# The first half's mix of two softmax maps: one DVE instruction, or a multiplication on ACT and an addition on POOL

## The chip, the cores and the metric

The kernel runs on one core of a Trainium2 chip. The core has five engines with queues of their own: PE (matrix products), DVE (vector), ACT (activations), POOL (general) and SP (here for DMA issues). An engine runs its instructions in the order in which they were issued to it, and waits on semaphores for what other engines produce. The metric is the device time of one execution in microseconds, as the median of several runs.

## The reference, cut to what matters

The block has two layers. Each projects 2048 latent and 256 context tokens, runs four mixers side by side (differential attention, HGRN2, windowed attention, mLSTM) and projects back. The change lies in the differential attention: 4 heads, and for each of them two softmax maps over all 2304 keys, which are subtracted before they meet the values:

```python
def attend(qs, ks, vs):
    s = jnp.einsum('mbhqd,mbhkd->mbhqk', qs, ks).astype(F32) * scale
    p = jax.nn.softmax(s, axis=-1)
    w = (p[0] - lam * p[1]).astype(vs.dtype)
    return jnp.einsum('bhqk,bhkv->bhqv', w, vs)

nb = n_tok // ATTN_QBLOCK
qb = jnp.moveaxis(q.reshape(2, b, DA_HEADS, nb, ATTN_QBLOCK, DA_QK), 3, 0)
o = lax.map(lambda qq: attend(qq, keys, vals), qb)
```

## The kernel before

A **unit** is 128 query rows of one head. There are 64 latent units in each layer, and in layer 0 also 8 context units over 256 keys. The 2304 keys of a latent unit are two halves: j = 0 with 1024 and j = 1 with 1280 columns (`HALF`). For each map m, first 1 and then 0:

- `diff_scores` has PE write the scores of a half into PSUM (`scr`), and DVE reduce it to its minimum (L1048). From the two minima DVE makes the bias of the map, called the **bound** here: for m = 1 a TENSOR_TENSOR of two columns of `sm` (in the trace under the helper's line, L108, as `sm<-sm 128x1`), for m = 0 a TENSOR_SCALAR (L1056).
- `diff_exp` has ACT take the exponential of both halves out of PSUM into `p`, with the row sums as accumulator (L105).
- `diff_mix`, for the unit before (`u1`), puts the maps together: j = 0 behind the bound of m = 1, j = 1 behind the bound of m = 0 (`tc.issue_after`). The factor `sm[:, 14:15]` comes out of three small DVE operations (L1073 to L1075). The mix itself was one DVE SCALAR_TENSOR_TENSOR, p1 * factor + p0 (L111). ACT casts the result to f16 (L1084), POOL subtracts that from the f32 value, which gives the low part (L108), and SP transposes both by DMA into `wt` (L1087).
- `diff_out` and `diff_norm` multiply `wt` with the values on PE, one and two units later, and normalise.

There is one score tile for each half (`sc0`, `sc1`, one buffer each), so PE can write the scores of the next map's half only when ACT has read the exponential of this half. Between them `pump` lets the projections of the other mixers run as filler on PE: `FSTEP` ns of it between the two halves' scores, `FGAP` behind the second. PE's order is written out by hand (`manual_schedule`); on DVE, ACT and POOL a scheduler sets the order of mix, exponentials, reductions and the filler's evictions.

A unit has two **rounds**: A from the bound of m = 1 to the bound of m = 0, B from there to the next unit's bound of m = 1.

Of the kernel before, what the change touches and what calls it, by code (L numbers as in the profile page):

```python
# [14 lines left out]
AF = mybir.ActivationFunctionType  # L15
ALU = mybir.AluOpType
# [57 lines left out]
def kernel(  # L74
# [8 lines left out]
    V, A, G, PE, SP = nc.vector, nc.scalar, nc.gpsimd, nc.tensor, nc.sync  # L83
# [20 lines left out]
    def act(o, i, f, **kw):  # L104
        A.activation(out=o, in_=i, func=f, **kw)  # L105

    def tt(e, o, a, b, op):
        return e.tensor_tensor(out=o, in0=a, in1=b, op=op)  # L108

    def stt(o, a, s, b, op0, op1):  # L110
        V.scalar_tensor_tensor(out=o, in0=a, scalar=s, in1=b, op0=op0, op1=op1)  # L111
# [146 lines left out]
    for l in range(n_layers):  # L258
# [83 lines left out]
        with tc.tile_pool(name=f"pa{l}", bufs=2, reuse_waits="tile", side="right" if l else "left") as pa, tc.tile_pool(name=f"pap{l}", bufs=4, space=PSUM, reuse_waits="tile") as pap:  # L342
# [53 lines left out]
            for gi, g in enumerate(gorder):  # L396
                g0, gn_ = GROUPS[g]
                n = gn_ // P
# [629 lines left out]
        with ExitStack() as st2:  # L1028
# [4 lines left out]
            def halves_of(u):  # L1033
                return [(2048, 256)] if u["ctx"] else HALF
# [33 lines left out]
            def diff_mix(u, j):  # L1068

                sm = u["sm"]  # L1070
                if j == 0:
                    zs = sm[:, 6:10].rearrange("p (m j) -> p m j", j=2)[:, :, :len(halves_of(u))]
                    V.tensor_reduce(sm[:, 10:12], zs, AX.X, ALU.add)  # L1073
                    V.reciprocal(sm[:, 12:14], sm[:, 10:12])
                    V.tensor_scalar(sm[:, 14:15], sm[:, 10:11], sm[:, 13:14], nlam, ALU.mult, ALU.mult)  # L1075
                    u["w"] = []
                hs = halves_of(u)
                if j >= len(hs):
                    return
                k0, n = hs[j]  # L1080
                p = u[1][j]
                stt(p[:, :n], p[:, :n], sm[:, 14:15], u[0][j][:, :n], ALU.mult, ALU.add)
                wl = u[0][j].bitcast(F16)
                A.copy(wl[:, :n], p[:, :n])  # L1084
                tt(G, wl[:, n:2 * n], p[:, :n], wl[:, :n], ALU.subtract)
                wt = da.tile([P, 20, P], F16, tag="wt", name="wt")
                SP.dma_start_transpose(wt[:, :2 * (n // P)], wl[:, :2 * n])  # L1087
                u["w"].append(wt)
# [80 lines left out]
            with tc.manual_schedule(engines=MANUAL):  # L1169
                while True:  # L1170
                    u = next(it, None)
                    if u is None and u1 is None and u2 is None and u3 is None:
                        break
                    if u:
                        diff_scores(u, 1)
                    if u3:
                        diff_out(u3, 1)
                    pump(FGAP * (u["work"] if u else 1.0))
                    if u1:
                        with tc.issue_after(u["nm"].ins) if u else ExitStack():  # L1180
                            diff_mix(u1, 0)
                    if u:
                        diff_exp(u, 1)
                    if u3:
                        diff_norm(u3, 0)
                    if u:
                        diff_scores(u, 0)
                    if u3:
                        diff_norm(u3, 1)
                    if u2:  # L1190
                        diff_out(u2, 0)
                    pump(FGAP * (u["work"] if u else 1.0))
                    if u1:
                        with tc.issue_after(u["nm"].ins) if u else ExitStack():
                            diff_mix(u1, 1)
                    if u:
                        diff_exp(u, 0)
                    u1, u2, u3 = u, u1, u2
# [528 lines left out]
```

## Time and profile before

| | |
|---|---|
| median of 3 runs | 4203.35 us (4197.22 to 4208.07) |
| the profiled execution's own time | 4220.02 us |
| its span in the profile | 4218.2 us |
| DVE / ACT / POOL busy | 2873.5 / 2332.9 / 2358.5 us |
| PE busy | 3570.4 us |
| instructions | 78854 |

The span runs from the first to the last instruction of the profiled execution; its own time has some 2 us around that. Busy times are sums over instructions, those that wait for a shared resource while they run included. The first scores of the attention stage start at 237.7 us and the last at 3295.9 us, with the other mixers of layer 0 and the first blocks of layer 1 between the two layers' stages.

### The profile page before, as it was taken

The numbers are of one execution on the slowest core, as the hardware profiler recorded it, in microseconds if no ns is written. First come the engines' busy times: TensorE is split into PE (matmuls) and PEld (weight loads), VectorE is DVE, ScalarE is ACT, GpSimd is POOL, SyncE is SP. The second block draws the span as 40 slices with busy tenths as digits, with TensorE's granted clock in tenths as the row PEclk, the third lists the DMA queues.
The fourth block names the chain that finished last, engine by engine and source line by source line (L and its number), as shares of the span: only waits on it lengthen the run. The fifth ranks groups of instructions, "written<-read, shape, count | busy, mean of one in ns | idle before, by whom it ended". The sixth has DMA issues, their size and how long they took to land.

```text
span 4218.2 us, 78854 instructions
## 1 busy us (share of the span) xinstructions
PE 3570.4 (85%) x30342; PEld 2395.7 (57%) x30342; DVE 2873.5 (68%) x4550; ACT 2332.9 (55%) x4679; POOL 2358.5 (56%) x1727
## 2 busy tenths in 40 slices
PE   6988878888769987989998888788876798789998
PEld 3656655444547675556656476544444575556665
DVE  5168888888885546556643499888899766556664
ACT  5245656666655545555653366666666664555663
POOL 4443555443445458778857545645344554677883
PEclk7999989999989986888999999999998999778998
DMA  5356866667666547467754467566776662646662
GB/s 205 100 138 151 189 131 165 135 150 157 127 142 165 134 133 174 143 167 170 184 152 142 121 133 158 126 147 150 151 161 132 155 163 84 166 124 161 169 169 76
DMA packets 1256960, 622.19 MB, mean 148 GB/s; under 512 B 913476, under 2 KB 1203848, under 8 KB 1256584
## 3 DMA queue, kind: packets, MB, share of 16 engines
q1 hardware_dynamic: 1154216, 490.64, 51.2%
q10 hardware_dynamic: 102368, 126.52, 8.9%
q8 instruction: 239, 3.92, 0.4%
q14 instruction: 137, 1.12, 0.1%
HBM read 291.76 MB, written 131.23 MB: 100 GB/s over the span
## 4 chain that ended last, share of the span: by engine, by line
PE 31%; DVE 18%; POOL 8%; issue 7%; DMA 7%; ACT 5%; SPq 1%; ACTq 0%; POOLq 0%; DVEq 0%
PE fx L94 7%; PE ptm L94 5%; PE pfm L94 5%; DVE sm L1048 4%; PE go L94 4%; PE mnum L94 3%; PE scr L94 2%; ACT p L105 2%; DVE p L111 2%; POOL E L108 2%; DMA swt<-ph 1%; POOL yt L108 1%; PE gA L94 1%; PE ss L94 1%; DVE sm L108 1%
## 5 line engine op out<-in xcount | busy, mean ns | idle before, releaser
L108 POOL TENSOR_TENSOR p<-p,p 128x1024 f16<-128x1024 f32 (+2 forms) x264 | 623.4, 2362 | 793.7 <-ACT p L1084 704.4
L94 PE MATMUL ptm<-wb,hh 128*128 128x256 f16 (+2 forms) x5024 | 834.6, 273 | 30.3 <-DVE tm L111 7.4
L105 ACT ACTIVATE p<-scr,sm 128x1024 f32<-128x1024 f32 (+2 forms) x528 | 628.2, 1194 | 416.4 <-DVE sm L1073 143.3
L1048 DVE TENSOR_REDUCE sm<-scr 128x1 f32<-128x1024 f32 (+2 forms) x528 | 698.9, 1326 | 218.0 <-PE scr L94 214.2
L94 PE MATMUL pfm<-hh,wb 128*128 128x512 f16 (+1 forms) x2592 | 809.0, 376 | 26.5 <-DVE gz L111 10.4
L94 PE MATMUL ptm<-wb,hl 128*128 128x256 f16 (+2 forms) x2512 | 671.9, 273 | 1.8 <-POOL hl L108 1.8
L94 PEld LDWEIGHTS <-wb 128*128 128x128 f16 x3888 | 378.8, 101 | 410.8 <-issue 81.1
L94 PE MATMUL scr<-Ks,Qs 128*128 128x512 f16 (+1 forms) x1296 | 364.5, 380 | 289.2 <-ACT p L105 284.1
L94 PEld LDWEIGHTS <-hh 128*128 128x128 f16 x5024 | 479.0, 100 | 131.3 <-issue 37.7
L94 PE MATMUL pfm<-hl,wb 128*128 128x512 f16 (+1 forms) x1296 | 488.1, 377 | 0.0
L111 DVE SCALAR_TENSOR_TENSOR p<-p,sm,p 128x1024 f32<-128x1024 f32 (+2 forms) x264 | 414.6, 1571 | 8.2
L94 PE MATMUL fx<-wo,mh 128*128 128x512 f16 x1088 | 371.8, 426 | 6.2 <-DVE xt L111 2.7
L94 PEld LDWEIGHTS <-Qs 128*128 128x128 f16 x1296 | 130.4, 102 | 429.9 <-issue 359.5
L1084 ACT CAST p<-p 128x1024 f16<-128x1024 f32 (+2 forms) x264 | 297.4, 1126 | 40.0 <-DVE p L111 35.3
L94 PEld LDWEIGHTS <-wt 128*128 128x128 f16 x4640 | 245.1, 103 | 71.7 <-DMA wt<-p 23.6
L94 PE MATMUL pv<-Vs,wt 128*128 128x128 f16 (+1 forms) x4640 | 259.6, 214 | 22.1 <-DMA wt<-p 14.6
L94 PEld LDWEIGHTS <-hl 128*128 128x128 f16 x2512 | 250.6, 100 | 36.1 <-POOL hl L108 3.3
L94 PE MATMUL fx<-wo,mlo 128*128 128x512 f16 x544 | 230.0, 423 | 6.1 <-DVE mlo L108 5.9
L108 POOL TENSOR_TENSOR E<-lk,cm 128x512 f32<-128x512 f32 (+1 forms) x136 | 205.3, 1510 | 41.2 <-DMA cm<-dhc 19.7
L108 POOL TENSOR_TENSOR ph<-swp,ph 128x640 f16<-128x640 f32 (+2 forms) x136 | 190.7, 1402 | 59.5 <-ACT ph L1326 45.1
L108 DVE TENSOR_TENSOR QQ<-hq,E 128x512 f32<-128x512 f32 x119 | 148.1, 1253 | 73.6 <-ACT E L105 35.9
L105 ACT ACTIVATE E<-E 128x1024 f32<-128x1024 f32 x136 | 143.0, 1052 | 99.5 <-POOL E L108 93.1
(298 smaller groups left out, 6853.7 us busy)
## 6 DMA issues: line engine op xcount, KB each, us to landing
wraw<-in_w_in_dram SPq DMA_DIRECT2D x60, 512.0 KB
dgt<-ga ACTq DMA_DIRECT2D x68, 256.0 KB
r1b<-dr SPq DMA_DIRECT2D x68, 256.0 KB
gtt<-dgt SPq DMA_DIRECT2D x34, 512.0 KB
mraw<-in_w_mod_dram SPq DMA_DIRECT2D x64, 256.0 KB
vi<-dhi SPq DMA_DIRECT2D x49, 256.0 KB
KSb<-dsk SPq DMA_DIRECT2D x56, 192.0 KB
Ks<-dka SPq DMA_DIRECT2D x64, 144.0 KB
```

The lines of the kernel that those rows point to most:

```text
L94: PE.matmul(o, lhsT=lhsT, rhs=rhs, start=start, stop=stop)
L105: A.activation(out=o, in_=i, func=f, **kw)
L108: return e.tensor_tensor(out=o, in0=a, in1=b, op=op)
L111: V.scalar_tensor_tensor(out=o, in0=a, scalar=s, in1=b, op0=op0, op1=op1)
L1048: V.tensor_reduce(sm[:, m * 2 + j:m * 2 + j + 1], ps[:, :n], AX.X, ALU.min)
L1084: A.copy(wl[:, :n], p[:, :n])
```

## The change

For the first half (j = 0) of a latent unit the DVE instruction is replaced by two: ACT multiplies p1 in place by the factor (`AF.Copy` with a scale of one value per partition), and POOL adds p0 to it. Both work on 128x1024 f32 in SBUF. The second half and the context units keep the DVE instruction. It happens 128 times.

```diff
--- before.py
+++ after.py
@@ -1079,7 +1079,11 @@
                     return
                 k0, n = hs[j]
                 p = u[1][j]
-                stt(p[:, :n], p[:, :n], sm[:, 14:15], u[0][j][:, :n], ALU.mult, ALU.add)
+                if j or u["ctx"]:
+                    stt(p[:, :n], p[:, :n], sm[:, 14:15], u[0][j][:, :n], ALU.mult, ALU.add)
+                else:
+                    act(p[:, :n], p[:, :n], AF.Copy, scale=sm[:, 14:15])
+                    tt(G, p[:, :n], p[:, :n], u[0][j][:, :n], ALU.add)
                 wl = u[0][j].bitcast(F16)
                 A.copy(wl[:, :n], p[:, :n])
                 tt(G, wl[:, n:2 * n], p[:, :n], wl[:, :n], ALU.subtract)
```

In the built programs DVE loses 128 instructions, ACT and POOL gain 128 each; on PE the order is the same through both attention stages. In the stages behind them (windowed attention, mLSTM and HGRN2), where the scheduler also orders PE, pieces of the two programs' order have changed places: nothing there was edited. Names such as `p_2591` are buffers of one unit's exponentials; the numbers differ between the two programs.

ACT in layer 0, from the exponential of a unit's map 1, half 0, to the cast of the unit before, half 1. Before:

```order
L105 ACTIVATE p_2745,sm<-scr,sm 128x1024
L105 ACTIVATE p_2747,sm<-scr,sm 128x1280
L1084 CAST p_2661<-p_2588 128x1024
L638 DMA dmv_100<-tm 128x256
L105 ACTIVATE p_2830,sm<-scr,sm 128x1024
L105 ACTIVATE p_2832,sm<-scr,sm 128x1280
L1084 CAST p_2663<-p_2590 128x1280
```

The two exponentials of a map follow each other, and the cast of the unit before comes behind them. The same place in the changed kernel:

```order
L105 ACTIVATE p_2749,sm<-scr,sm 128x1024
L105 ACTIVATE p_2591<-p_2591,sm 128x1024
L105 ACTIVATE p_2751,sm<-scr,sm 128x1280
L638 DMA dmv_100<-tm 128x256
L1088 CAST p_2664<-p_2591 128x1024
L105 ACTIVATE p_2834,sm<-scr,sm 128x1024
L105 ACTIVATE p_2836,sm<-scr,sm 128x1280
L1088 CAST p_2666<-p_2593 128x1280
```

The multiplication (`p_2591<-p_2591,sm`) stands between the two exponentials of map 1, and the cast of its result comes behind the second of them. So it stands in 78 of the 128 units.

A place of the other kind, also on ACT in layer 0, in the changed kernel:

```order
L105 ACTIVATE p_7010,sm<-scr,sm 128x1024
L162 COPY mrow<-modps 128x256
L105 ACTIVATE p_7012,sm<-scr,sm 128x1280
L105 ACTIVATE p_6876<-p_6876,sm 128x1024
L105 ACTIVATE ot<-pv,sm 128x64
L105 ACTIVATE p_7061,sm<-scr,sm 128x1024
L105 ACTIVATE p_7063,sm<-scr,sm 128x1280
L162 COPY mrow<-modps 128x256
L1088 CAST p_6950<-p_6876 128x1024
L1088 CAST p_6952<-p_6878 128x1280
```

Here the multiplication (`p_6876<-p_6876,sm`) stands behind both exponentials of map 1, and the cast of its result behind the exponentials of map 0, next to the cast of the second half. So it is in 43 units; in the last 7 the cast follows the multiplication with no exponential of map 0 between them.

POOL in layer 0, the low parts of three units. Before:

```order
L108 TENSOR_TENSOR p_2361<-p_2297,p_2361 128x1024
L108 TENSOR_TENSOR p_2363<-p_2299,p_2363 128x1280
L108 TENSOR_TENSOR p_2498<-p_2418,p_2498 128x1024
L108 TENSOR_TENSOR p_2500<-p_2420,p_2500 128x1280
L108 TENSOR_TENSOR p_2661<-p_2588,p_2661 128x1024
L108 TENSOR_TENSOR p_2663<-p_2590,p_2663 128x1280
```

One subtraction of 1024 columns and one of 1280 alternate. And in the changed kernel:

```order
L108 TENSOR_TENSOR p_2420<-p_2420,p_2500 128x1024
L108 TENSOR_TENSOR p_2500<-p_2420,p_2500 128x1024
L108 TENSOR_TENSOR p_2502<-p_2422,p_2502 128x1280
L108 TENSOR_TENSOR p_2591<-p_2591,p_2664 128x1024
L108 TENSOR_TENSOR p_2664<-p_2591,p_2664 128x1024
L108 TENSOR_TENSOR p_2666<-p_2593,p_2666 128x1280
```

Each addition (`p_2591<-p_2591,p_2664`) stands ahead of the subtraction of the same half on POOL's queue.

## Rows read from the trace of the kernel before

**Rows 1.** Page, part 1: busy us of each engine, share of span, instructions.

```profile
PE 3570.4 (85%) x30342; PEld 2395.7 (57%) x30342; DVE 2873.5 (68%) x4550; ACT 2332.9 (55%) x4679; POOL 2358.5 (56%) x1727
```

**Rows 2.** Windows in the attention stage: length, busy us (instructions) by engine, clock, DMA.

```profile
800.00:1200.00 400.00, 316.22 (x2607) 195.13 (x2606) 343.52 (x545) 242.10 (x394) 169.12 (x96) 0.93 0.64 142
...
2800.00:3200.00 400.00, 321.57 (x2651) 187.74 (x2651) 351.15 (x502) 259.82 (x401) 177.99 (x93) 0.96 0.71 153
```

**Rows 3.** Waits, whole span: waiting line, releaser: us in total, times, longest.

```profile
POOL p L108 <- ACT p L1084: 704.4, 194, 12.7
...
PE scr L94 <- ACT p L105: 284.1, 190, 6.9
DVE sm L1048 <- PE scr L94: 214.2, 261, 4.7
...
ACT p L105 <- DVE sm L1056: 141.7, 68, 7.5
```

**Rows 4.** Timeline of DVE, one unit: start, duration us, line, operation, [idle before].

```profile
3022.74 0.15 DVE L108 TENSOR_TENSOR sm<-sm 128x1 f32<-128x1 f32 x1
...
3023.57 1.28 DVE L111 SCALAR_TENSOR_TENSOR p<-p,sm,p 128x1024 f32<-128x1024 f32 x1
3024.87 1.23 DVE L1048 TENSOR_REDUCE sm<-scr 128x1 f32<-128x1024 f32 x1
3026.71 1.49 DVE L1048 TENSOR_REDUCE sm<-scr 128x1 f32<-128x1280 f32 x1 [0.61 <-PE scr L94]
3028.23 0.27 DVE L1056 TENSOR_SCALAR sm<-sm,shf 128x1 f32<-128x1 f32 x1
3028.42 1.57 DVE L111 SCALAR_TENSOR_TENSOR p<-p,sm,p 128x1280 f32<-128x1280 f32 x1
...
3032.26 1.49 DVE L1048 TENSOR_REDUCE sm<-scr 128x1 f32<-128x1280 f32 x1 [0.61 <-PE scr L94]
...
3033.86 1.04 DVE L108 TENSOR_TENSOR sm<-sm 128x1 f32<-128x1 f32 x1
```

**Rows 5.** Timeline of ACT, the same unit.

```profile
3022.99 1.11 ACT L105 ACTIVATE p<-scr,sm 128x1024 f32<-128x1024 f32 x1 [0.68 <-DVE sm L1073]
...
3024.09 1.32 ACT L105 ACTIVATE p<-scr,sm 128x1280 f32<-128x1280 f32 x1
...
3025.39 1.04 ACT L1084 CAST p<-p 128x1024 f16<-128x1024 f32 x1
3026.33 0.69 ACT L105 ACTIVATE fm<-pfm,bcol 128x512 f32<-128x512 f32 x1
...
3028.54 1.12 ACT L105 ACTIVATE p<-scr,sm 128x1024 f32<-128x1024 f32 x1 [1.52 <-DVE sm L1056]
...
3029.65 1.32 ACT L105 ACTIVATE p<-scr,sm 128x1280 f32<-128x1280 f32 x1
...
3030.95 1.25 ACT L1084 CAST p<-p 128x1280 f16<-128x1280 f32 x1
```

**Rows 6.** Timeline of PE, the same unit, scores alone.

```profile
3024.24 0.59 PE L94 MATMUL scr<-Ks,Qs 128*128 128x512 f16 x2 [0.34 <-ACT p L105]
...
3025.97 0.70 PE L94 MATMUL scr<-Ks,Qs 128*128 128x512 f16 x3
```

**Rows 7.** Timeline of POOL, the same unit.

```profile
3026.51 2.13 POOL L108 TENSOR_TENSOR p<-p,p 128x1024 f16<-128x1024 f32 x1 [4.52 <-ACT p L1084]
3032.28 2.61 POOL L108 TENSOR_TENSOR p<-p,p 128x1280 f16<-128x1280 f32 x1 [3.64 <-ACT p L1084]
```

**Rows 8.** Groups by form: count, busy us, mean ns, idle us before, releasers.

```profile
L111 DVE SCALAR_TENSOR_TENSOR p<-p,sm,p 128x1024 f32<-128x1024 f32 x128 | 174.0, 1359 | 7.6
...
L1084 ACT CAST p<-p 128x1024 f16<-128x1024 f32 x128 | 133.5, 1043 | 28.0 <-DVE p L111 23.3 <-DVE gates L637 1.8 <-issue 1.4
...
L108 POOL TENSOR_TENSOR qe<-qe,hq 128x1024 f32<-128x1024 f32 x17 | 40.4, 2378 | 51.7 <-ACT qe L105 51.7
```

**Rows 9.** Tile sm: count, duration ns min/median/max, first and last start.

```profile
L108 DVE TENSOR_TENSOR sm<-sm x136: 127/773/2320, 248.7 to 3290.6; 128x1 f32<-128x1 f32 x136
```

## The prediction

> **What bounds the kernel now.** The page's first part comes first: PE is busy for 85% of the span, DVE for 68% [rows 1]. That is an average over stages, so the next view is the windows in the attention stage, where the change lies: there DVE is busy for 344 and 351 of 400 us, PE for 316 and 322, ACT for 242 and 260, POOL for 169 and 178 [rows 2]. DVE at 86 to 88% looks like the bound, and POOL looks empty. The waits say something else: DVE's reductions of the scores waited 261 times for PE, out of 528 (136 units, two maps, two halves, fewer halves for context units), and PE's scores waited 190 times, 284 us in all, for ACT's exponentials [rows 3]. So the three engines chase each other in a ring, and none is the bound alone.
>
> The ring is best seen in one unit with little filler on DVE [rows 4 to 7]. I count from the end of the bound of map 1, 3022.89. ACT starts the first exponential at 3022.99 and the second at 3024.09, which ends at 3025.41. PE's scores for the second half start at 3025.97. DVE's reduction of them starts at 3026.71, after 0.61 us of waiting for exactly these scores, and the bound of map 0 ends at 3028.50. Round A took 5.61 us, and DVE's mix (3023.57, 1.28 us) was no part of its chain: DVE was idle behind it. In round B the chain is another: ACT's exponentials end at 3030.97, the cast of the second half runs from 3030.95, POOL's subtraction from 3032.28 to 3034.89, and the bound of the next unit, a DVE operation on two SBUF columns, takes 1.04 us instead of the 0.15 us that it took one unit earlier: it ends at 3034.90, when POOL's instruction ends. Round B took 6.40 us. So POOL's subtraction holds this bound up. That is common: over the span the median of this operation is 773 ns against a minimum of 127 [rows 9].
>
> **The change, part by part.** *DVE loses* 128 mixes of 1359 ns mean [rows 8], 174 us. In the unit above that gives nothing, since the wait for scores only grows from 0.61 us. It gives something where the reduction found its scores ready, about half the time (267 of 528, by the count above), so in some 64 rounds A. There the gain lies between 0 and 1.36 us; half or more of these rounds belong to units where ACT's delay below brings the scores later anyway, so I take 0.3 us each, near the lower end: **-20 us** (bounds 0 and -87).
>
> *ACT gains* 128 multiplications of 128x1024 f32. The trace has none with a scale from a tile; the nearest row is the cast of the same tile, 1043 ns [rows 8], and back to back with the next instruction it took 0.94 us (3025.39 to 3026.33); the exponential out of PSUM took 1.11 [rows 5]. I take 1.0 us of delay (bounds 0.94 and 1.11). In 78 units the built order puts it between the two exponentials of map 1. Then the second ends at 3026.41 instead of 3025.41. PE's filler had kept the scores waiting until 3025.97 anyway; they can now start about 0.14 us behind the exponential (as the scores of 3024.24 did, whose exponential ended at 3024.10), at 3026.55. So 0.58 us of the 1.0 reaches the reduction, which already waited, and round A grows by that: 78 x 0.58 = **+45 us** (bounds: 0 if PE's filler is long enough everywhere, 78 x 1.11 = 87).
>
> The Trainium skill has a price for such an instruction (page "ScalarE: Activation LUTs", section "What ACT_TABLE_LOAD costs"): about 280 ns and 0.833 ns per column with an operand per partition, an estimate of 1133 ns for 1024 columns. No row here shows a multiplication of this kind; the exponential, with a bias per partition, agrees with 1.11 us [rows 5]. By the page the delay would be 0.09 us more than the cast's 1.04, this term 52 and the sum below 70 in place of 63.
>
> *POOL gains* 128 additions. The nearest row is an f32 product of the same shape, 2378 ns [rows 8], the subtraction with an f16 side took 2.13 [rows 7]; I take 2.38. In the 78 units: the multiplication ends at 3025.13, the addition runs from 3025.21 (0.08 us behind, as the subtraction of 3026.51 was behind its cast) to 3027.59. ACT's cast, behind the second exponential, must now wait for it and runs from 3027.65 to 3028.69, and the subtraction from 3028.77 to 3030.90. Queued behind that waiting cast on ACT are evictions of filler (0.69 us here) and the exponential of map 0, which is due only at 3029.12; so the cast itself costs no chain. The subtraction does. The mix of the second half, which stays on DVE and reads two SBUF tiles, wants to start at about 3029.1, and meets POOL's subtraction as the bound of 3033.86 did. It can start at 3030.90 and ends at 3032.47, where without the subtraction in its way it would have ended at 3029.99 + 0.58 = 3030.57. The cast of the second half was ready for it at 3031.53 and now starts 0.95 us later, POOL's second subtraction follows it, and the next unit's bound, which ends with that subtraction, is 0.95 us later too. DVE's reductions, delayed as much, come to 3035.24 and are still ahead of that end. So round B grows by 0.95 us wherever this bound is the last wait. I count that in 58% of the units: in 74 of 128 the DVE operation is stretched and its companion is POOL's `p<-p,p`; the others' rounds end in filler. 78 x 0.58 x 0.95 = **+43 us** (bounds: 0 if the mix slips in ahead of the subtraction, 78 x 0.95 = 74 if every round ends there).
>
> *In 43 units* the multiplication stands behind both exponentials, where ACT sat idle for 1.52 us [rows 5], so round A stays. The cast of the first half moves behind the exponentials of map 0, to 3030.95, its subtraction to 3032.07 to 3034.20, and the cast and the subtraction of the second half behind these. The bound wants to start at about 3033.8. POOL's instruction then ends at 3034.20 and not at 3034.89, and the bound gets in between the two: -0.6 us, in the same 58%: 43 x 0.58 x 0.6 = **-15 us**. If it had to wait for the second one as well, the sign would turn: 2.6 us later.
>
> *In 7 units* the cast follows the multiplication with only filler between. It waits for the addition until 3028.9, ends at 3030.0, and the exponential behind it, due at 3028.54, waits: 7 x 1.4 = **+10 us**.
>
> The additions also delay the rest on POOL's queue; nothing on SP's queue is added, and the transposes of the first half, 2 us later, feed products of the next unit, a unit's length away. The stages behind the attention got another order without an edit; no row prices that. I take 0, with 20 us to either side (1% of the roughly 2000 us outside the two attention stages).
>
> The sum is -20 + 45 + 43 - 15 + 10 = **+63 us**. Against the profiled execution's own 4220 that is 4283; that execution ran 17 us over the median of 4203, so on the median's side I forecast **4266 us**. Below 0.3% (13 us) a change of this kernel can't be told from none.
>
> **The rivals.**
>
> *DVE is the bound after all* (other side, faster). At 88% busy, every round that carries filler on DVE would end with DVE's own queue. Against it speak the 261 waits for scores; for it that the other half did not wait. If the full 1.36 us come back in those 64 rounds A, that is -87 us, and ACT's delay is hidden behind DVE's queue: 4116 us. It decides from where fewer than some 30 of 128 reductions of round A wait for their scores in the changed kernel. The Trainium skill's page "Perfetto Trace Analysis", section "Optimizing Scalar/DVE Operations", speaks for this rival: where DVE is saturated, moving work to the scalar engine or even GpSimd may pay, with the warning that the latter shares a port with DVE. By that rule the time falls; the trace agrees with the warning (1.04 us instead of 0.15).
>
> *ACT's delay alone.* The mix of the second half comes late enough to miss the subtraction, as filler often makes it, and round B does not grow: 45 + 10 - 15 - 20 = +20, 4223 us.
>
> *PE's filler hides it all.* Filler before the second half's scores covers the whole 1.0 us in most units, and the two small gains cancel the rest: no change, 4203 us.
>
> *POOL and its lock are the bound everywhere.* Every unit of the 78 pays both rounds in full and DVE's relief gives nothing: 78 x (0.58 + 0.95) + 10 = +129, 4332 us.
>
> **How the numbers follow.** My forecast's case gets 0.45, DVE as bound 0.17, ACT alone 0.16, no change 0.11, POOL everywhere 0.11. Slower by over 0.3% are the forecast, ACT alone (+0.47%) and POOL everywhere, 0.72; within it is "no change", 0.11; faster is 0.17. The range of 4190 to 4340 us holds all but the faster rival, with the 20 us of the reordered stages within it; the likeliest case's own range is 4230 to 4305.
>
> **What would show it.** Right: in the attention windows DVE's busy time falls by clearly less than the mixes' 174 us in sum, because the mix of 128x1280 stretches by a few hundred ns over its mean; the wait of the 1280-column reduction for scores grows; ACT's second exponential starts some 1 us later after the first; the cast of the first half waits for POOL. Wrong: PE's idle time before scores shrinks and the units get shorter; or the two attention stages keep their length and the difference lies in the stages behind them.

## The result and the profile after

The changed kernel takes 4354.84 us (median of 4 runs, 4346.61 to 4370.72) against 4200.28 us of the kernel before beside it (4186.67 to 4208.07): ratio 1.0362, 95% interval 1.0329 to 1.0395. The forecast was 4266 us with a range to 4340: slower, as forecast, but by two and a half times the forecast's 63 us, and outside the range. The profiled execution took 4362.06 us, its span is 4360.3, so 142 us more than before; the two profiled executions are compared below.

Page of the changed kernel, part 1, which answers to [rows 1]:

```profile
PE 3609.1 (83%) x30342; PEld 2422.0 (56%) x30342; DVE 2828.8 (65%) x4422; ACT 2477.6 (57%) x4807; POOL 2666.1 (61%) x1855
```

DVE lost 174 us of mixes and its busy time fell by 45 only. Most of the rest is in the groups by form (count, busy us, mean ns, idle us before, releasers), to be held against [rows 8, 9]. Two groups of the kernel before:

```profile
L111 DVE SCALAR_TENSOR_TENSOR p<-p,sm,p 128x1280 f32<-128x1280 f32 x128 | 234.2, 1830 | 0.0
...
L108 DVE TENSOR_TENSOR sm<-sm 128x1 f32<-128x1 f32 x136 | 97.5, 717 | 0.6
```

The changed kernel:

```profile
L1048 DVE TENSOR_REDUCE sm<-scr 128x1 f32<-128x1280 f32 x256 | 380.7, 1487 | 160.1 <-PE scr L94 159.3
...
L1048 DVE TENSOR_REDUCE sm<-scr 128x1 f32<-128x1024 f32 x256 | 312.4, 1220 | 210.1 <-PE scr L94 209.4
L111 DVE SCALAR_TENSOR_TENSOR p<-p,sm,p 128x1280 f32<-128x1280 f32 x128 | 303.6, 2372 | 0.1
L108 POOL TENSOR_TENSOR p<-p,p 128x1024 f32<-128x1024 f32 x128 | 302.7, 2365 | 305.2 <-ACT p L105 300.5 <-DMA mraw<-in_w_mod_dram 2.4 <-DMA Ks<-dka 1.2
...
L105 ACT ACTIVATE p<-p,sm 128x1024 f32<-128x1024 f32 x128 | 146.2, 1143 | 8.5 <-DVE sm L1075 8.3
...
L1088 ACT CAST p<-p 128x1024 f16<-128x1024 f32 x128 | 133.7, 1045 | 75.3 <-POOL p L108 67.3 <-DVE sm L1056 2.5 <-issue 2.4
...
L108 DVE TENSOR_TENSOR sm<-sm 128x1 f32<-128x1 f32 x136 | 108.7, 799 | 0.9
```

The mix of the second half, which the change doesn't touch, went from a mean of 1830 ns to 2372: 69 us in sum. The bound of map 1 went from a mean of 717 ns to 799, 11 us in sum. What is left is spread over groups that the change doesn't touch, none of them longer by more than 18 us. The new addition on POOL takes 2365 ns (the forecast took 2380), the new multiplication on ACT 1143 ns (it took 1.04 us for its row and 1.0 of delay). The Trainium skill (page "ScalarE: Activation LUTs", section "What ACT_TABLE_LOAD costs") gave an estimate of 1133 ns; the trace agrees, and it was nearer than the cast. The prediction's sum by this price is off: it adds 0.09 us to a delay of 1.0, though the price lies 0.13 above that, so the term would be 56 and not 52, and the sum 74 and not below 70.

The waits over the whole span (waiting line, releaser: us, times, longest), against [rows 3]:

```profile
DVE sm L1048 <- PE scr L94: 386.6, 311, 6.1
...
PE scr L94 <- ACT p L105: 355.4, 244, 6.6
...
ACT p L1088 <- POOL p L108: 67.3, 64, 3.9
```

DVE's wait for scores grew from 214.2 to 386.6 us, 172 us, almost the 174 us that it was relieved of. PE's wait for ACT's exponentials grew from 284.1 to 355.4. That the 172 us lie so close to the 174 is chance: over the whole span DVE's idle time grew by 187 us, 142 by the longer span and 45 by less work. So the relief did not shorten the program; it became idle time.

Where in the program the 142 us lie: the row of the tile `sm` (count, min/median/max ns, first and last start), which answers to [rows 9]:

```profile
L108 DVE TENSOR_TENSOR sm<-sm x136: 135/758/2574, 247.8 to 3432.3; 128x1 f32<-128x1 f32 x136
```

From the first bound to the last it was 3041.9 us and is 3184.5; behind the last it was 927.6 and is 928.0. All of it lies in the attention stages and between them: 996 to 1052 us in layer 0, 898 to 971 in layer 1, 1148 to 1161 in the stage between. I measured each round of each unit in both traces, from the end of one bound to the end of the next (units in the same order; 134 rounds of each kind, without the last unit of each layer):

| rounds by the place of ACT's multiplication | round A, sum | round B, sum |
|---|---|---|
| between the exponentials of map 1 (77) | +54 us (+0.70 each) | +45 us (+0.59 each) |
| behind both (40) | -13 (-0.33 each) | +26 (+0.65 each) |
| ahead of both (6) | +16 (+2.6 each) | -1 |
| in a context unit's round, or no multiplication (11) | -4 | +11 |

That is +133 of the 142 us; 9 lie outside these rounds.

The third kind was not seen ahead of the prediction. By the trace's order on ACT the 128 multiplications stand 78 times between the exponentials of map 1, 43 times behind them (two of these in a context unit's round) and 7 times ahead of the first. These 7 are the ones described there by their cast; the prediction has ACT's next exponential wait for the cast in them. What happens is that both exponentials of map 1 wait for the multiplication: in one such round it runs at 2940.71, the first exponential at 2941.77, and round A is 7.17 us where it was 5.62. In five of the 43 the cast stands ahead of map 0's exponentials, not behind them.

The unit of [rows 4 to 7] in the changed kernel; its bound of map 1 ends at 3146.13. Timeline of DVE:

```profile
3145.98 0.15 DVE L108 TENSOR_TENSOR sm<-sm 128x1 f32<-128x1 f32 x1
...
3148.11 1.23 DVE L1048 TENSOR_REDUCE sm<-scr 128x1 f32<-128x1024 f32 x1 [1.40 <-PE scr L94]
3150.57 1.49 DVE L1048 TENSOR_REDUCE sm<-scr 128x1 f32<-128x1280 f32 x1 [1.23 <-PE scr L94]
3152.09 0.27 DVE L1056 TENSOR_SCALAR sm<-sm,shf 128x1 f32<-128x1 f32 x1
3152.28 3.25 DVE L111 SCALAR_TENSOR_TENSOR p<-p,sm,p 128x1280 f32<-128x1280 f32 x1
3155.45 2.61 DVE L1048 TENSOR_REDUCE sm<-scr 128x1 f32<-128x1024 f32 x2
...
3158.17 1.35 DVE L108 TENSOR_TENSOR sm<-sm 128x1 f32<-128x1 f32 x1
```

Timeline of ACT:

```profile
3146.22 1.11 ACT L105 ACTIVATE p<-scr,sm 128x1024 f32<-128x1024 f32 x1 [0.68 <-DVE sm L1073]
...
3147.33 1.14 ACT L105 ACTIVATE p<-p,sm 128x1024 f32<-128x1024 f32 x1
3148.37 1.32 ACT L105 ACTIVATE p<-scr,sm 128x1280 f32<-128x1280 f32 x1
...
3150.92 1.05 ACT L1088 CAST p<-p 128x1024 f16<-128x1024 f32 x1 [0.57 <-POOL p L108]
...
3155.56 1.26 ACT L1088 CAST p<-p 128x1280 f16<-128x1280 f32 x1 [0.65 <-DVE p L111]
```

Timeline of POOL:

```profile
3148.54 2.35 POOL L108 TENSOR_TENSOR p<-p,p 128x1024 f32<-128x1024 f32 x1 [3.34 <-ACT p L105]
3152.05 2.13 POOL L108 TENSOR_TENSOR p<-p,p 128x1024 f16<-128x1024 f32 x1 [1.16 <-ACT p L1088]
3156.90 2.61 POOL L108 TENSOR_TENSOR p<-p,p 128x1280 f16<-128x1280 f32 x1 [2.72 <-ACT p L1088]
```

This is the forecast's chain step by step. The second exponential starts 2.15 us behind the first, not 1.10; the 1280-column reduction waits 1.23 us for its scores, not 0.61; round A is 6.24 us, +0.63 (forecast +0.58). The addition holds the cast back to 3150.92, the cast the subtraction to 3152.05 to 3154.18. The mix of the second half is issued at 3152.28, 0.23 us into that subtraction, and stands to 3155.53: the 3.25 us are 1.9 of waiting and some 1.4 of work. Both reductions of the next unit's map 1 (in one row, x2) then run with no wait, and its bound meets POOL's last subtraction and ends with it at 3159.5. Round B is 7.16 us, +0.76 (forecast +0.95).

### The profile page after: what moved, and what is told of

Same layout as the page of the kernel before. It is cut to its first block, busy times and chain, and to the rows that moved or that the text cites. A ratio compares the mean times of both kernels' runs of the same rounds, so it can differ in the third digit from the quotient of the medians.

```text
span 4360.3 us, 78928 instructions
## 1 busy us (share of the span) xinstructions
PE 3609.1 (83%) x30342; PEld 2422.0 (56%) x30342; DVE 2828.8 (65%) x4422; ACT 2477.6 (57%) x4807; POOL 2666.1 (61%) x1855
## 5 line engine op out<-in xcount | busy, mean ns | idle before, releaser
L108 POOL TENSOR_TENSOR p<-p,p 128x1024 f32<-128x1024 f32 (+3 forms) x392 | 930.7, 2380 | 674.1 <-ACT p L1088 366.3
L1048 DVE TENSOR_REDUCE sm<-scr 128x1 f32<-128x1024 f32 (+2 forms) x528 | 697.8, 1325 | 388.1 <-PE scr L94 386.6
L94 PE MATMUL ptm<-wb,hh 128*128 128x256 f16 (+2 forms) x5024 | 847.0, 276 | 25.7 <-DVE tm L111 6.8
L94 PE MATMUL scr<-Ks,Qs 128*128 128x512 f16 (+1 forms) x1296 | 371.6, 387 | 357.5 <-ACT p L105 355.4
L111 DVE SCALAR_TENSOR_TENSOR p<-p,sm,p 128x1280 f32<-128x1280 f32 (+1 forms) x136 | 310.1, 2280 | 0.7
L105 ACT ACTIVATE E<-E 128x1024 f32<-128x1024 f32 x136 | 142.9, 1052 | 70.6 <-POOL E L108 65.8
```

Source lines behind the costliest of these rows:

```text
L94: PE.matmul(o, lhsT=lhsT, rhs=rhs, start=start, stop=stop)
L1048: V.tensor_reduce(sm[:, m * 2 + j:m * 2 + j + 1], ps[:, :n], AX.X, ALU.min)
```

## The experiments

Each time is the median of 4 to 10 runs, with the ratio to the kernel before, measured beside it, and its 95% interval; the kernel before had a median of 4200 to 4207 us beside each. Rounds A and B are compared with those of the kernel before as in the table above, over all 134 where no units are named.

### ACT's delay alone

**An identity multiplication** on ACT in the kernel before, between the two exponentials of map 1 in all 128 units:

```diff
+                    if m and not j and not u["ctx"]:
+                        u["cp"] = act(p[:, :n], p[:, :n], AF.Copy, scale=one_t)
```

> Kernel before, plus one ACT multiplication by 1.0, in place on the exponential of map 1, half 0, pinned ahead of the second exponential of map 1 in all 128 latent units; DVE and POOL keep their work. Theory (ACT's delay in round A and POOL's hold on two-input DVE operations in round B add up): the delay alone costs what round A grew by in the 78 units of the change, 0.65 us, in all 128: +83, about 4283 us. Rival 'POOL alone': the delay is hidden by PE's filler, 4200 us, within 13.

4289.03 us, ratio 1.0184 (1.0146 to 1.0221). Rounds A grew by 69 us in sum, 0.54 for each of the 128; rounds B fell by 12. The size of the step holds, with DVE's mix still in its place.

**The same instruction behind the second exponential**:

> As the kernel with an ACT multiplication by 1.0 between the two exponentials of map 1, with that multiplication pinned behind the second exponential instead. The same ACT work, off the way of the scores. Theory (ACT's place costs, not its load): 4206, up to +20. Rival 'ACT's load costs': 4289 as with the multiplication between them.

4244.00 us, ratio 1.0098 (1.0067 to 1.0130): between the two expectations, nearer to the first but beyond its 20 us. Rounds A are free of it (-0.08 us each), as forecast for the units with the late place. Rounds B grew by 0.30 us each: the cast of the first half comes a microsecond later, its subtraction with it, and the mix of the second half takes 2305 ns in the mean.

### POOL's hold on DVE

**POOL's first subtraction issued twice** in the kernel before, so that POOL has more work at that place and ACT has none:

```diff
+                if j == 0 and not u["ctx"]:
+                    tt(G, wl[:, n:2 * n], p[:, :n], wl[:, :n], ALU.subtract)
```

> Kernel before, with POOL's subtraction of the first half (128x1024, two SBUF inputs, 2.13 us) issued twice in a row in the 128 latent units, the second time with the same result; ACT, DVE and the order of all else unchanged, and no cast waits for POOL. Theory (POOL's hold on the 1280-column mix lengthens round B): the second one runs where that mix wants to start; the mix is stretched as in the kernel with the addition on POOL (mean 2.4 us instead of 1.83) and the time rises by 70 to 120 us, 4275 to 4325. Rival 'the chain multiplication, addition, cast is what costs, not the hold': 4206, within 13.

4323.65 us, ratio 1.0278 (1.0251 to 1.0305). Rounds B +0.63 us each, rounds A +0.19. Groups by form:

```profile
L108 POOL TENSOR_TENSOR p<-p,p 128x1024 f16<-128x1024 f32 x256 | 625.4, 2443 | 458.0 <-ACT p L1084 432.6 <-issue 18.3
...
L111 DVE SCALAR_TENSOR_TENSOR p<-p,sm,p 128x1280 f32<-128x1280 f32 x128 | 272.9, 2132 | 0.0
...
L108 DVE TENSOR_TENSOR sm<-sm 128x1 f32<-128x1 f32 x136 | 111.4, 819 | 0.5
```

The mix and the bound both stretch with no edit of theirs, from 1830 and 717 ns.

**POOL's extra work at another time**: two additions of 256 columns (665 ns each), ready when DVE reduces out of PSUM:

```diff
+                if j == 0 and not u["ctx"]:
+                    for k in range(2):
+                        tt(G, p[:, 1024:], p[:, k * 256:k * 256 + 256], p[:, k * 256:k * 256 + 256], ALU.add)
```

> Kernel before, plus two POOL additions of 128x256 (about 0.68 us each, two SBUF inputs) on the mixed first half, into columns of its tile that nothing reads, issued ahead of the first half's subtraction in the latent units. POOL gets 1.36 us more work a unit, but at a time when DVE reduces scores out of PSUM, and it is done before the subtraction is due. Theory (what costs is POOL's hold on DVE operations with two SBUF inputs, so the time at which POOL works): 4206, up to +20 where filler moves them. Rival 'POOL's load costs': in proportion to the doubled subtraction (118 us for 2.13 us), +75, about 4280.

4230.01 us, ratio 1.0064 (1.0041 to 1.0086): a little over the first expectation and far below the rival. It is less POOL work than an addition (1.33 us of 2.37), so it bounds the effect and doesn't settle its size.

**The bound as a reduction** of the columns between, so that DVE has one SBUF input:

```diff
-                    u["nm"] = tt(V, sm[:, 5:6], sm[:, o:o + 1], sm[:, o2:o2 + 1], ALU.min)
+                    u["nm"] = V.tensor_reduce(sm[:, 5:6], sm[:, o:o2 + 1], AX.X, ALU.min)
```

In the kernel before:

> Kernel before, with the bound of map 1 made by a TENSOR_REDUCE over the two columns (one SBUF input) in place of the TENSOR_TENSOR (two). Theory: the bound no longer waits for POOL (mean 0.72 us, 0.15 its own), part of it comes back as a wait elsewhere, as in the changed kernel, where the same edit gave 52 us of the 83 that stood there: about -45, 4160 us. Rival 'the wait only moves': 4206, within 13.

4165.95 us, ratio 0.9904 (0.9871 to 0.9936): faster than both kernels. Groups by form:

```profile
L1054 DVE TENSOR_REDUCE sm<-sm 128x1 f32<-128x2 f32 x128 | 18.5, 145 | 0.3
```

145 ns in the mean where the two-input form took 717. Rounds B fell by 0.40 us each. The same edit in the changed kernel:

> Changed kernel, with the bound of map 1 made by a TENSOR_REDUCE over the two columns (one SBUF input) in place of a TENSOR_TENSOR (two SBUF inputs); same order on every engine. Theory: this bound no longer waits for POOL's running instruction (mean 0.8 us in the changed kernel, some 0.15 of it its own): about -0.65 us in 128 units, 4270 us. Rival 'the hold costs nothing, another wait ends there': 4355 us, within 13.

4302.98 us, ratio 1.0237 (1.0209 to 1.0265): 52 us less than the changed kernel, not the 85 expected. Units with the late multiplication: rounds B -0.26 us against before, where they had +0.65. Units with the early one: +0.07, where they had +0.59. But with the reduction in both kernels the change still costs 4303 against 4166, 137 us; between these two, rounds A of the early kind differ by 0.84 us each and rounds B by 0.42. The bound is the last wait of round B; behind it stand the reductions, late because the mix was held (2447 ns here), and they can be the next wait when the bound is free. The two traces bear this out in part: from the held mix to the bound DVE runs without a gap in 44 of the 77 early units, in the kernel before with the same bound in 14 of the same 77. It was not tried by itself.

### One half of the change

**The multiplication on DVE**, the addition on POOL as in the change (so ACT is free of it):

```diff
-                    act(p[:, :n], p[:, :n], AF.Copy, scale=sm[:, 14:15])
+                    V.tensor_scalar(p[:, :n], p[:, :n], sm[:, 14:15], None, ALU.mult)
```

> Changed kernel, with the multiplication on DVE instead of ACT; the addition stays on POOL. Theory: round A stays as before, but the subtraction of the first half still comes late and holds the 1280-column mix and the next bound: +0.6 us in 128 units, about 4277 us. Rival 'ACT alone': 4200 us. Rival 'DVE relief counts': under 4190, since DVE's multiplication is shorter than its mix.

4322.43 us, ratio 1.0279 (1.0256 to 1.0302). Rounds A -0.01 us each, rounds B +0.69. So ACT's delay is gone, and POOL's part costs 116 us without it, 93 of them in rounds B (the mix of 1280 columns takes 2503 ns); I had expected 77. DVE's multiplication:

```profile
L1085 DVE TENSOR_SCALAR p<-p,sm 128x1024 f32<-128x1024 f32 x128 | 108.3, 846 | 7.8
```

**The addition on DVE**, the multiplication on ACT as in the change:

```diff
-                    tt(G, p[:, :n], p[:, :n], u[0][j][:, :n], ALU.add)
+                    tt(V, p[:, :n], p[:, :n], u[0][j][:, :n], ALU.add)
```

> Changed kernel, with the addition on DVE instead of POOL; the multiplication stays on ACT (between the exponentials in 67 units, built order). POOL's queue is that of before. Theory: only ACT's delay is left, 67 x 0.65 = +44, about 4245 us, and the mix of 1280 columns goes back to its mean of before, 1830 ns. Rival 'POOL alone': 4200. Rival 'ACT alone': as much as the change, 4330 or more.

4367.41 us, ratio 1.0393 (1.0360 to 1.0427): a miss by 122 us. It isn't the change less POOL, since a new wait comes in. Waits:

```profile
ACT p L1088 <- DVE p L108: 117.3, 89, 4.2
```

The addition stands in DVE's queue among the reductions, and ACT's cast waits for it; in 58 units that cast stands right behind the multiplication with map 0's exponentials queued behind it. This run therefore tells nothing on the price of POOL.

### All multiplications behind both exponentials

**In the changed kernel** the mix's two instructions and the cast are issued behind the second exponential:

```diff
-                    if u1:
-                        with tc.issue_after(u["nm"].ins) if u else ExitStack():
-                            diff_mix(u1, 0)
...
+                    if u1:
+                        with (tc.issue_after(u["nm"].ins) if u else ExitStack()), (tc.issue_after(u["ex"].ins) if u else ExitStack()):
+                            diff_mix(u1, 0)
```

> Changed kernel, with the multiplication pinned behind the second exponential of map 1 in every unit, so that it is never between the two. Theory: round A goes back to that of before; round B costs what it cost in the 43 units of this kind in the changed kernel, 0.6 us, and a few units more where the cast waits: 128 x 0.6 = +77, about 4285 us. Rival 'ACT's place is the whole cause': 4206. My forecast's step (-0.6 us in 58% of such units): under 4180.

4376.45 us, ratio 1.0408 (1.0379 to 1.0436): a miss, and slower than the change itself. In the 124 units with a late multiplication rounds A grew by 0.42 us each, B by 0.69. Waits:

```profile
PEld L94 <- DMA wt<-p: 100.9, 46, 8.6
...
PE pv L94 <- DMA wt<-p: 75.5, 38, 8.1
...
ACT p L105 <- DMA wt<-p: 48.8, 39, 3.0
...
ACT p L105 <- POOL p L108: 42.9, 36, 3.0
```

The cast then stands behind the exponentials of map 0 in 98 of the 128 units, and everything behind it ends about a round later. A buffer of `p` (four to a map, two units' worth) is then still being read by POOL's subtraction or the transposes when the exponential that writes into it is due: the third wait was 4.2 us in sum in the kernel before, and the fourth has no row there.

**With the bound as a reduction on top**:

> The kernel with the late multiplication, and with the bound of map 1 as a TENSOR_REDUCE. Theory: what the late multiplication costs is a bound that misses the gap between POOL's two subtractions; without that wait round B falls to about 5.8 us in clean units: 4120 to 4180 us, below the kernel before and near the kernel before with the same bound. Rival 'POOL's queue bounds round B by itself': 4230 or more.

4361.44 us, ratio 1.0363 (1.0330 to 1.0396): a miss as well. In the same 124 units rounds B are down to +0.06 us and rounds A up to +0.75; the exponentials' wait for POOL to free `p` is 78.3 us in sum, up from 42.9.

### DVE's relief alone

**The kernel before without the first half's mix**:

```diff
-                stt(p[:, :n], p[:, :n], sm[:, 14:15], u[0][j][:, :n], ALU.mult, ALU.add)
+                if j or u["ctx"]:
+                    stt(p[:, :n], p[:, :n], sm[:, 14:15], u[0][j][:, :n], ALU.mult, ALU.add)
```

> Kernel before without the first half's mix in the latent units: DVE's 128 operations of 1359 ns are left out and nothing takes their place, so the output lacks that part (the first half's map 0). It prices DVE's relief by itself. My forecast's step: -20, 4186 us. Rival 'DVE is the bound': -87 or more, under 4120. Theory now: 0 to -20, since in the units of the changed kernel with the late multiplication round A's mean did not change.

4269.67 us, ratio 1.0164 (1.0120 to 1.0209): slower by 63 us with less work, a miss. The order on ACT says why: with no mix to wait for, the scheduler put the cast of the first half directly behind its own unit's exponentials of map 0, in 122 units behind both of them. That is earlier than before, where 119 of these casts stand behind the next unit's exponentials of map 1. In most units it then stands directly ahead of the cast of the second half of the unit before, which now comes later. Timeline of one unit:

```profile
2899.16 4.70 POOL L108 TENSOR_TENSOR p<-p,p 128x1024 f16<-128x1024 f32 x2 [7.62 <-ACT p L1085]
...
2911.44 1.33 ACT L105 ACTIVATE p<-scr,sm 128x1280 f32<-128x1280 f32 x1 [2.56 <-DMA wt<-p]
...
2912.76 2.19 ACT L1085 CAST p<-p 128x1024 f16<-128x1024 f32 x2
```

Both casts and both subtractions (x2), of two units, stand together, the first half's ahead, and the exponential at 2911.44 waits 2.56 us for a transpose to free its buffer.

**Half of the mix**, 512 of the 1024 columns, which keeps the cast's place in 118 units:

```diff
+                else:
+                    stt(p[:, :512], p[:, :512], sm[:, 14:15], u[0][j][:, :512], ALU.mult, ALU.add)
```

> The kernel before, whose DVE mix of the first half covers only the first 512 of the 1024 columns; the mix of the other columns is left out, so its output lacks them. DVE loses about half of the mix, some 0.64 us of 1.28 in each of 128 units, 82 us in sum. Without the whole mix the cast of the first half had moved behind the exponentials of map 0 in most units, next to the second half's cast; here it stands behind the second exponential of map 1 in 118 units, as in the kernel before (119). If the loss without the mix (+69 us) came from that place of the cast, and the relief of DVE itself is worth little, the time is that of before or a little less: 4190 to 4205 us. If the relief is worth what the forecast put on it, half of 20 us, it is 4193. If taking DVE work out of round A costs time by itself (the bound then meets POOL more often), half of the 69 us shows: 4235.

4192.09 us (10 runs) against 4200.55 (13): ratio 0.9981 (0.9959 to 1.0003). With the order kept, half the relief gives about 8 us, which just can't be told from none; so the loss of the run without the mix goes with the place of the cast.

## Why the forecast was wrong in size

The four signs that the prediction named for its being right are all there: DVE's busy time, the stretched mix, the second exponential a microsecond later, the cast that waits for POOL.

**ACT's delay in round A** was forecast at +45 us and measured at +54 in the units with the early multiplication, 0.70 us each instead of 0.58. The identity multiplication shows it as a cause by itself.

**POOL's hold in round B** was forecast at +43 and measured at +45 in the same units. Mechanism and sum were right. The working put 0.95 us on 58% of the units; it was 0.59 in the mean over all. The double subtraction and the multiplication on DVE show that POOL's work ahead of the mix costs this without ACT; the run with POOL's work at another time speaks for the meeting with DVE and against POOL's load, with less work than the addition. One thing I had not seen: the bound isn't needed for it. Where it never waits, rounds B of these units still differ by 0.42 us, most likely because the reductions behind the held mix then end the round.

**The units with the late multiplication** are the step that failed: "the bound gets in between the two: -0.6 us, in the same 58%", -15 us; measured +26 in their rounds B. The step named the condition under which its sign turns, "If it had to wait for the second one as well", and gave it no share. Two units of the changed kernel show both sides. DVE:

```profile
2846.48 2.24 DVE L108 TENSOR_TENSOR sm<-sm 128x1 f32<-128x1 f32 x1
...
3072.22 0.30 DVE L108 TENSOR_TENSOR sm<-sm 128x1 f32<-128x1 f32 x1
```

POOL, the two subtractions of the same units back to back (x2):

```profile
2844.01 4.70 POOL L108 TENSOR_TENSOR p<-p,p 128x1024 f16<-128x1024 f32 x2 [0.28 <-ACT p L1088]
...
3070.37 4.72 POOL L108 TENSOR_TENSOR p<-p,p 128x1024 f16<-128x1024 f32 x2 [0.84 <-ACT p L1088]
```

At 3072.22 the first subtraction is still running; the bound ends with it at 3072.5, ahead of the second one, and round B is 5.76 us where it was 6.45. At 2846.48, behind two other operations of DVE's queue, the second subtraction has run since 2846.1 (2844.01 and the 2.13 us of [rows 7]): the bound ends with it at 2848.7, and round B is 8.32 where it was 6.45. The Trainium skill states the lock behind it (page "SBUF — State Buffer", section "Who interferes with whom"): who issues first has the shared pair for the whole instruction, and a DVE operation with two SBUF inputs needs it. The trace agrees: both waits end with a POOL instruction. By ends of the bound, 12 of the 40 rounds end with the first subtraction (-0.99 us each, -0.7 in the median; -12 us), 18 with the second (+1.39, +25), and 10 with neither (+1.27, +13). Against the kernel before, with the bound as a reduction the 18 go from +25 us to -9 and the 12 from -12 to -15, while the 10 stay at +14. So the loss of the 18 is the bound's wait for the second subtraction; what lengthens the 10 is open.

**DVE's relief** was forecast at -20 us, and no run shows it clear of noise. Half of the mix removed by itself gave 8 us, in line with the term's half of 10. In the changed kernel rounds A with the late multiplication are 13 us shorter, but the same rounds are 14 us shorter with the identity multiplication behind the second exponential, where DVE keeps its mix: so it is not the relief. Two of these rounds that go from 8.17 to 6.47 us and from 9.01 to 6.54 take 6.48 and 6.52 in that run. With the early multiplication rounds A grew no less than with the mix in place (0.70 us against 0.52 in the same rounds with the identity multiplication). The term also counted too many rounds: in round A 49 of the 128 reductions of 1280 columns found their scores ready, not 64.

**The 7 units** with +10 came to +14 in the six that could be measured, by another way than forecast (the multiplication ahead of both exponentials). **The stages outside** gave +9, within the 20 us allowed; they moved by -25 to +24 us in experiments that had no edit there.

By terms: the late units' rounds B are 41 of the 79 us that the forecast missed on the profiled execution, rounds A of the early kind 9, rounds with no multiplication or in context units, for which the forecast had no term, 11 in B, the stages 9; the rest adds up to 9. The medians are 155 us apart and not 142: the profiled execution of the kernel before was 20 us over the median of 4200, that of the changed kernel 7 over its own.

Of the rivals, DVE as the bound, ACT's delay alone and filler that hides all are excluded by the growth of both rounds; for the first of them fewer than 30 of 128 reductions of round A should have waited for scores, and 99 did (79 before). "POOL and its lock are the bound everywhere", 4332 us, was the nearest number by another way: the units of the early kind did not pay in full, and the late kind paid too. TensorE's granted clock, in the mean over the span, was 0.901 of full speed before and 0.894 after, and a score matmul took 381 and 387 ns in the mean: over all 1296 that is 8 us, as an estimate, so the clock is not the cause. A range that let the late units' sign turn (43 units at +1.2 or more, +52 in place of -15) would have reached 4333 from the likeliest case and beyond 4340 with the stages; it should have.

What stays open: the 10 late rounds above, and how the end of round B passes from the bound to the reductions. For the late units the loss was tested with the bound's form, not with the cast held in its old place.

## What to carry to other kernels

Work moved off a busy engine is worth only the time in which nothing else was late: here DVE lost 174 us of mixes, its wait for scores grew by 172, and the two engines that took the work stood on the chain that DVE waits for. Before work is given to POOL, look for DVE operations with two SBUF inputs at the same place, small ones above all; a 128x1 operation stood for 2.2 us, and rewriting it as a reduction gained 1%, where the offload lost 3.6%. And where a scheduler orders the engines, look where the instructions behind the edit land: the kernel without the mix lost 63 us with one cast in another place, and the kernel with half of it, the cast in its old place, lost nothing.

## What the runs showed of the hardware

- The bound, a DVE operation with two SBUF inputs, was let in between two POOL subtractions that stand back to back where it was issued during the first one (12 rounds; 3072.22, ended with the first); issued during the second one, it ended with the second (18 rounds; 2.24 us at 2846.48).
- A TENSOR_REDUCE over two SBUF columns took 144 and 145 ns in the mean of 128, beside the same POOL work in which the two-input form took 717 to 799. The Trainium skill (page "SBUF — State Buffer", section "Who interferes with whom") says that a reduction never contends on this chip; the trace agrees.
- DVE's multiplication by a per-partition factor (TENSOR_SCALAR, 128x1024 f32, SBUF to SBUF) took 846 ns, the mix with its second input 1359, POOL's f32 addition of the same shape 2365 and ACT's multiplication 1143, all as means with the other engines at work.
